# A two-layer hybrid attention kernel on one core: the last pair's reciprocals on another DMA queue, two exponentials always on ACT, three lasting value tiles, one-column Newton steps as tensor_scalar

## The chip, the core and the metric

One Trainium2 chip; the kernel runs on one of its cores. A core has five engines that run side by side and wait for each other through semaphores: PE (TensorE, matmuls), DVE (VectorE, elementwise work), ACT (ScalarE, activations and casts), POOL (GpSimd, elementwise work here) and SP (SyncE, which here only issues DMAs). ACT can issue DMAs too. Each engine takes its instructions strictly in order, and so does each DMA queue's issuer: an instruction that waits holds up all that stand behind it on its engine. The metric is the device time of one execution in microseconds (us), as the median of several runs.

## The reference, cut to what matters

Two transformer layers over 1024 tokens of width 1024, in fp32. Layer 0 mixes with 12 heads of forgetting attention and 4 heads that attend to a memory of 256 rows; layer 1 with 12 latent-attention (MLA) heads and the same 4 memory heads. Each layer ends with an output projection and a convolutional feed-forward network (FFN).

```python
def rmsnorm(x, g):
    xf = x.astype(jnp.float32)
    y = xf * lax.rsqrt(jnp.mean(xf * xf, axis=-1, keepdims=True) + EPS)
    return (y * g.astype(jnp.float32)).astype(x.dtype)
...
    for i in range(DEPTH):
        h = rmsnorm(x, norm_mix[i])
        ...            # p = h @ w_in; o_mix: softmax attention per head, causal
        o_mem = memory_cross(p[..., -MEM_WIDTH:], k_mem, v_mem, mem_q_gain[i], mem_k_gain[i])
        x = x + jnp.concatenate([o_mix, o_mem], axis=-1) @ w_out[i]
        x = x + conv_ffn(rmsnorm(x, norm_ffn[i]), ffn_w_up[i], ffn_conv_w[i], ffn_conv_b[i],
                         ffn_w_down[i])
```

Two pieces matter here. The softmax of a head is exp(score - max) divided by its sum, and the kernel divides after the product with the values. The rmsnorm ahead of each FFN needs one reciprocal square root for every token.

## The kernel before, in words

PE multiplies in a reduced fp32 format (fp32r), so every operand is kept as a high part (the value rounded to fp32r) and a low part (what the rounding lost), and one product is three matmuls. `split` makes the parts: a cast on ACT (L83) and a subtraction on DVE or POOL (L90).

**Attention** (`attention`, 16 heads in 8 pairs per layer). For a group of scores in PSUM (tile `psS`, two buffers), `probs` forms the probabilities: `pf`, the exponential in fp32; `ph`, the same in fp32r; and `plo`, their difference, on POOL. A counter, `pl.turn`, sets who makes `ph`: in four groups of five (layer 0) or five of six (layer 1) ACT computes the exponential twice from PSUM, `ph` first; in the others ACT computes `pf` and DVE casts it. There are 160 groups, 80 in each layer. Each head's values are in `vh` and `vl`; `vh` has a 65th column of ones, which gives the softmax sum as one more output row. In layer 0 `vtile` takes a new pair of tiles for each of the 12 heads from a pool of three and writes the ones anew (L1349).

When both heads of a pair are done, `evacuate` has their outputs in one tile (`oh`) and the sums in `sums`. `norm1` takes the reciprocals (DVE, L387), writes them to DRAM (`rec`, L388) and reads them back as rows spread over 64 partitions each (`rrow`, two DMAs, L391). `norm2` multiplies (L93) and `split_out` makes the high and low parts `oth` and `otl`. All DMAs of `norm1` are issued by SP, behind whatever else stands on its queue.

**Output projection** (`out_proj`). PE multiplies all eight pairs with `wo_w`, the split output weights, which come in as `wo_raw` (two buffers) for one half of the columns and then the other. The first half is arranged so that the last pair comes last. The old x (eight tiles of 512 KB) is loaded at the same time. `add` (L692) adds a result to x, and in the second half calls `ffn.ready`: for each of eight token tiles t, in the order 0, 4, 1, 5, 2, 6, 3, 7, ACT sums the squares, `rsqrt` takes the reciprocal root, and L248 scales.

**rsqrt** works on DVE alone: L216, L217 (a first guess by bit arithmetic), L219, and three Newton steps of two instructions each. With a width of one column, 32 times in the program, they are two `scalar_tensor_tensor`, L222 and L226; each has two tensors in SBUF among its inputs.

**FFN** (`FFN.run`). It transposes the scaled x on PE block by block and splits the blocks (`f_B`, `f_T`), while POOL makes the low parts of weight operands (`f_op`). Then PE is fed steadily.

The order on each engine is made by a scheduler from priorities and its own model of durations. It also hands eight DMA completion counters (lanes, named DMAHW0 to DMAHW7) to the DMAs in turn, over all queues: a DMA waits until the DMA that had its lane before it has landed.

Of the kernel before, what the change touches and what calls it, by code (L numbers as in the profile page):

```python
# [8 lines left out]
F32R = mybir.dt.float32r  # L9
BF16 = mybir.dt.bfloat16  # L10
I32 = mybir.dt.int32
AF = mybir.ActivationFunctionType
OP = mybir.AluOpType
# [4 lines left out]
P = 128  # L18
D = 1024
S = 1024  # L20
NT = S // P
# [53 lines left out]
def hybrid_kernel(ctx: ExitStack, tc: tile.TileContext, A, out):  # L75
    nc = tc.nc
# [4 lines left out]
    def copy(eng, o, i):  # L81
        if eng == "a":
            nc.scalar.copy(o, i)  # L83
        elif eng == "v":
            nc.vector.tensor_copy(o, i)
        else:
            nc.gpsimd.tensor_copy(o, i)

    def sub(eng, o, a, b):
        (nc.vector if eng == "v" else nc.gpsimd).tensor_tensor(o, a, b, op=OP.subtract)  # L90
# [43 lines left out]
    def open_pool(name, bufs, **kw):  # L134
        return tc.alloc_tile_pool(name=name, bufs=bufs, reuse_waits="tile", **kw)
# [7 lines left out]
    rec_d = dram.tile([2, 8, 2, S], F32, name="rec")  # L143
# [62 lines left out]
    def gc(key, n):  # L206
        i = GC[key]
        return g_cols[0:n, i:i + 1]


    def rsqrt(ss, n, width):

        v = small.tile([P, 32], F32, name="rs_v")[:, :width]
        y = small.tile([P, 32], F32, name="rs_y", bufs=6)[:, :width]
        t = small.tile([P, 32], F32, name="rs_t")[:, :width]
        nc.vector.tensor_scalar(v, ss, 1.0 / n, EPS, op0=OP.mult, op1=OP.add)  # L216
        nc.vector.tensor_scalar(y.bitcast(I32), v.bitcast(I32), -0.5, 1597463007.0, op0=OP.mult, op1=OP.add)  # L217
        if width == 1:
            nc.vector.tensor_scalar(v, v, -0.5, None, op0=OP.mult)  # L219
        for i in range(3):  # L220
            if width == 1:
                nc.vector.scalar_tensor_tensor(t, y, y, v, op0=OP.mult, op1=OP.mult)  # L222
            else:
                nc.vector.tensor_tensor(t, y, y, op=OP.mult)
                nc.vector.scalar_tensor_tensor(t, t, -0.5, v, op0=OP.mult, op1=OP.mult)
            nc.vector.scalar_tensor_tensor(y, t, 1.5, y, op0=OP.add, op1=OP.mult)  # L226
        return y

    def sumsq(acc, src, n):
# [3 lines left out]
    class Norm:  # L233
# [5 lines left out]
        def stats(self, *ts):  # L239
            ss = small.tile([P, 4], F32, name="n_ss", bufs=3)  # L240
            for i, t in enumerate(ts):
                sumsq(ss[:, i:i + 1], self.src(t), D)
            y = rsqrt(ss[:, :len(ts)], D, len(ts))
            for i, t in enumerate(ts):
                self.r[t] = y[:, i:i + 1]
# [15 lines left out]

    pl = Pools()
    pl.mem_rows = set()
    pl.turn = 0

    def slot(name="slot", dt=F32):
        return pl.slots.tile([P, 1024], dt, name=name, tag="slot")
# [11 lines left out]
    def attention(L, heads, leads, offset=0, bg=None, fill={}):  # L279
# [30 lines left out]
        def score_units(h, g):  # L310
            half, parts = h.groups[g]
            state = {}

            def part(i):
                if i == 0:
                    state["ps"] = psS()
                ps = state["ps"]
                kt, q0, n, off = parts[i]
                passes = h.passes(kt, q0, n)
                for j, (l, r) in enumerate(passes):  # L320
                    mm(ps[:, off:off + n], l, r, j == 0, j == len(passes) - 1)
                if h.causal and q0 == kt * P:
                    mm(ps[:, off:off + P], idb, mS, False, True)
                if i == len(parts) - 1:
                    pend.append((h, g, *probs(ps, off + n)))

            return [lambda i=i: part(i) for i in range(len(parts))]

        def probs(ps, w):
            pf = pl.pf.tile([P, 1024], F32, name="pf")[:, :w]  # L330
            ph = pl.p.tile([P, 1024], F32R, name="ph")[:, :w]
            plo = pl.p.tile([P, 1024], F32R, name="plo", bufs=pl.nplo)[:, :w]
            pl.turn += 1
            if pl.turn % pl.dve_turn:
                nc.scalar.activation(ph, ps[:, :w], AF.Exp)  # L335
                nc.scalar.activation(pf, ps[:, :w], AF.Exp)  # L336
            else:
                nc.scalar.activation(pf, ps[:, :w], AF.Exp)
                copy("v", ph, pf)
            sub("p", plo, pf, ph.bitcast(F32))  # L340
            return ph, plo

# [42 lines left out]
        def norm1(r):  # L385
            rec = small.tile([16, P], F32, name="rec", bufs=2)
            nc.vector.reciprocal(rec, pl.sum[r])  # L387
            nc.sync.dma_start(rec_d[L, r].rearrange("b (j p) -> (b j) p", p=P), rec)  # L388
            pl.rows[r] = slot("rrow")
            for b in range(2):  # L390
                nc.sync.dma_start(pl.rows[r][64 * b:64 * b + 64, :], rec_d[L, r, b:b + 1, :].to_broadcast([64, S]))  # L391

        def norm2(r, half):
            raw = pl.OT[r]
# [82 lines left out]
    class Head:  # L477
# [6 lines left out]
        def qk_tiles(self):  # L484
            i = pl.nqk % len(pl.qk)
            pl.nqk += 1
            self.QA, self.KA, self.QB, self.KB = T = pl.qk[i]
            if self.causal and i not in pl.rows_set:
                pl.rows_set.add(i)
                for j, a, b in self.const_rows:  # L490
                    copy(self.rows_eng[len(pl.rows_set) > 1], T[j][a:b, :], ones1[a:b, 0:1].to_broadcast([b - a, S]))
# [8 lines left out]
    def load_pair(T, odd, Th, Tl, tl0, tl1, gcol, half):  # L500

        hs = slice(half * 512, half * 512 + 512)
        if odd:
            px = T[0:HD, hs]
        else:
            px = psX()
            for i in range(4):
                t = half * 4 + i
                transpose(px[:, i * P:(i + 1) * P], T[:, t * P:(t + 1) * P], ident)
            copy("v" if pl.layer else "a", T[0:HD, hs], px[HD:P, :])  # L510
            px = px[0:HD, :]
        split_T(px, Th, Tl, tl0, tl1, gcol, HD, half)
# [7 lines left out]
    def dup(dst, src):  # L520
        nc.sync.dma_start(dst.bitcast(F32), src.bitcast(F32))

    class FoxHead(Head):
# [7 lines left out]
        def prep(self):  # L531
            self.qk_tiles()
            o = (self.row % 2) * HD
            q, k = self.p
            QA, KA, QB, KB = self.QA, self.KA, self.QB, self.KB

            def qt(half):
                load_pair(q, self.row % 2, QA, QB, 0, 64, gc("fox_q", HD), half)
                if half:
                    dup(QB[64:128, :], QA[0:64, :])  # L540

            def kt(half):
                if not half:
                    dup(KA[64:66, :], self.cum[self.row:self.row + 1])
                load_pair(k, self.row % 2, KA, KB, 64, 128, gc("fox_k", HD), half)
                if half:
                    dup(KB[0:64, :], KA[0:64, :])

            def vs():
                self.vh, self.vl = pl.vtile()  # L550
                v = self.pv.rearrange("p (t j) -> p t j", t=NT)[:, :, o:o + HD]
                copy("a", self.vh[:, :, 0:64], v)
                sub("p" if self.row < 2 else "v", self.vl, v, self.vh[:, :, 0:64].bitcast(F32))

            return [lambda: kt(0), lambda: qt(0), lambda: kt(1), lambda: qt(1), vs]
# [635 lines left out]
    def pair(c, W, extra=()):  # L1191
# [4 lines left out]
        for t in range(NT):  # L1196
# [17 lines left out]
            for f in extra[:n]:  # L1214
                f()
            del extra[:n]
        r = rsqrt(ss.rearrange("p t i -> p (t i)"), HD, 32).rearrange("p (t i) -> p t i", t=NT)
        for i, T in ((0, q), (2, k)):
            Tv = T.rearrange("p (t h d) -> p t h d", t=NT, h=2)
# [120 lines left out]
    for p in (wp, wr, hp):  # L1340
        p.release()

    qkp, vp = open_pool("qk0", 1), open_pool("v0", 3)
    pl.pf, pl.p, pl.nplo = open_pool("pf0", 2), open_pool("p0", 3), 3

    def vtile():
        vh = vp.tile([P, NT, 65], F32R, name="vh")
        vl = vp.tile([P, NT, 64], F32R, name="vl")
        nc.vector.tensor_copy(vh[:, :, 64], ones1[:, 0:NT])  # L1349
        return vh, vl  # L1350

    pl.vtile = vtile
    pl.OTs = {}

    def split_out(r):
# [3 lines left out]

    pl.split_out = split_out  # L1360
    qk_tiles(qkp, (1, 2, 0), 3)
    pl.ev, pl.dve_turn = "v", 5
    fox = [FoxHead(h, QKV[h // 2][0], QKV[h // 2][1], cum) for h in range(NH)]
    mem = [MemHead(h, 0, mq0) for h in range(NMH)]
    rest = attention(0, fox + mem, [2] * 16, offset=tc.cur_priority - p_last)
# [42 lines left out]
    with early(ffn.p_tail):  # L1408
# [4 lines left out]
        for d in range(ND):  # L1413
            raw = ffn.rp.tile([P, ND, P], F32, name="f_raw").rearrange("p a b -> p (a b)")[:, :N1 + N2]
            nc.sync.dma_start(raw, mwin[d * P:(d + 1) * P, :])
            w = w1.tile([P, 2, N1 + N2], F32R, name="w1_w")
# [221 lines left out]
    def swap():  # L1638
# [3 lines left out]
        for p in (w1, xtp, hp):  # L1642
# [6 lines left out]

    fill = {2: [swap], 5: [lambda: g0.project(2)], 6: [lambda: latents_T(6)],  # L1650
            10: [lambda: g0.project(3), lambda: g0.squares(1), lambda: g0.rotate(1), g0.scale_k, g0.scale_q]}
    pl.ev, pl.dve_turn = "a", 6
    mk = [slot("mK", F32R).rearrange("p (h i) -> p h i", h=NMH) for i in range(2)]

    ORDER = [12, 13, 14, 15, 0, 1, 2, 3, 4, 5, 6, 7, 8, 9, 10, 11]
# [1 line left out]
    heads = [MemHead(r - NH, 1, mq1) if r >= NH else MlaHead(r) for r in ORDER]  # L1657
# [7 lines left out]
    for g in range(1, 6):  # L1665
        p = groups[g].pieces()
# [37 lines left out]
    for j in range(6):  # L1704
        i, x = divmod(t0 + 0.1 + 0.28 * j, 1.0)
# [48 lines left out]
```

## Time and profile before

| | |
|---|---|
| median of 3 runs | 2599.51 us (2595.33 to 2603.27) |
| the profiled execution's own time | 2597.95 us |
| its span, first to last instruction | 2596.2 us |
| PE busy | 2391.8 us, 92% |
| DVE busy | 1819.7 us, 70% |
| POOL busy | 1546.4 us, 60% |
| ACT busy | 1203.2 us, 46% |
| chain that ended last | PE 47%, DVE 34%, ACT 6%, DMA 4% |

PE is busy nearly throughout, so time can be won only where PE stands idle or runs at its lower clock, and there the chain shows who kept it waiting. The idle stretches are few: the start, the two attentions (near 285 to 530 and 1430 to 1800 us), the joints between attention and output projection (near 560 and 1836 us), and the starts of the two FFNs (620 to 680 and 1884 to 1940 us).

### The profile page before, as it was taken

The numbers are of one execution on the slowest core, as the hardware profiler recorded it, in microseconds if no ns is written. First come the engines' busy times: TensorE is split into PE (matmuls) and PEld (weight loads), VectorE is DVE, ScalarE is ACT, GpSimd is POOL, SyncE is SP. The second block draws the span as 40 slices with busy tenths as digits, with TensorE's granted clock in tenths as the row PEclk, the third lists the DMA queues.
The fourth block names the chain that finished last, engine by engine and source line by source line (L and its number), as shares of the span: only waits on it lengthen the run. The fifth ranks groups of instructions, "written<-read, shape, count | busy, mean of one in ns | idle before, by whom it ended". The sixth has DMA issues, their size and how long they took to land.

```text
span 2596.2 us, 32544 instructions
## 1 busy us (share of the span) xinstructions
PE 2391.8 (92%) x11609; PEld 1960.3 (76%) x11609; DVE 1819.7 (70%) x2937; ACT 1203.2 (46%) x2341; POOL 1546.4 (60%) x992
## 2 busy tenths in 40 slices
PE   8999899888999999989998798979989999997999
PEld 7999666667777777767888576757767777776787
DVE  7422788738777677779877868773576776678786
ACT  5544777613444444433454555554254444443343
POOL 1122476723577777678941556665157777776797
PEclk9999899998999999989999899989989999999999
DMA  5210122252222222441330110012312222225221
GB/s 161 59 50 26 34 59 59 61 172 83 66 78 77 90 73 80 180 156 38 106 130 11 34 31 18 19 37 90 132 54 85 73 81 82 82 73 235 81 98 65
DMA packets 163653, 208.91 MB, mean 80 GB/s; under 512 B 11175, under 2 KB 124682, under 8 KB 163490
## 3 DMA queue, kind: packets, MB, share of 16 engines
q1 hardware_dynamic: 162054, 206.63, 25.1%
q8 instruction: 92, 1.51, 0.2%
q14 instruction: 71, 0.58, 0.1%
q10 hardware_dynamic: 1436, 0.18, 0.0%
HBM read 153.34 MB, written 39.98 MB: 74 GB/s over the span
## 4 chain that ended last, share of the span: by engine, by line
PE 47%; DVE 34%; ACT 6%; issue 5%; DMA 4%; POOL 2%; SPq 1%; ACTq 0%; DVEq 0%; POOLq 0%
PE psX L102 19%; PE psS L102 17%; DVE f_v L883 11%; PE psO L102 10%; DVE f_v L93 4%; POOL f_op L90 2%; ACT f_v L881 2%; PE psX L106 2%; ACT f_v L886 2%; DMA rrow<-rec 1%; DVE f_S L781 1%; DVE mA L292 1%; DVE f_S L1071 1%; ACT f_op L83 1%; DVE f_u L849 1%
## 5 line engine op out<-in xcount | busy, mean ns | idle before, releaser
L90 POOL TENSOR_TENSOR f_op<-f_S,f_op 128x512 fp32r<-128x512 f32 x248 | 364.3, 1472 | 287.3 <-ACT f_op L83 287.2
L102 PE MATMUL psS<-f_T,f_op 128*128 128x512 f32 x1584 | 384.6, 394 | 31.1 <-DVE f_u L849 26.1
L90 POOL TENSOR_TENSOR plo<-pf,ph 128x1024 fp32r<-128x1024 f32 (+2 forms) x160 | 313.8, 1972 | 164.6 <-ACT pf L336 99.5
L102 PEld LDWEIGHTS psS<-f_T,f_op 128*128 128x128 f32 x1584 | 293.0, 188 | 106.2 <-issue 38.6
L83 ACT CAST f_op<-f_S 128x512 fp32r<-128x512 f32 x248 | 153.5, 621 | 330.4 <-PE psS L102 143.7
L102 PE MATMUL psX<-f_B,f_op 128*128 128x512 f32 x1260 | 296.0, 389 | 0.0
L102 PEld LDWEIGHTS psX<-f_B,f_op 128*128 128x128 f32 x1260 | 236.5, 188 | 49.2
L90 POOL TENSOR_TENSOR f_op<-f_raw,f_op 128x512 fp32r<-128x512 f32 x146 | 229.1, 1583 | 30.7 <-ACT f_op L83 30.2
L102 PE MATMUL psS<-f_op 128*128 128x512 f32 x960 | 228.1, 396 | 11.2 <-DVE f_x L1128 8.6
L102 PEld LDWEIGHTS psS<-f_op 128*128 128x128 f32 x960 | 182.6, 191 | 53.4 <-DVE f_x L1128 10.3
L883 DVE SCALAR_TENSOR_TENSOR f_v<-f_cg,cw,f_v 128x1023 f32<-128x1023 f32 x88 | 164.0, 1864 | 54.4 <-ACT f_v L881 52.8
L102 PE MATMUL psX<-f_op 128*128 128x512 f32 x666 | 175.7, 406 | 25.9 <-DVE f_op L90 17.8
L90 POOL TENSOR_TENSOR f_op<-f_d,f_op 128x512 fp32r<-128x512 f32 x118 | 175.0, 1502 | 25.4 <-ACT f_op L83 25.1
L102 PEld LDWEIGHTS psX<-f_op 128*128 128x128 f32 x666 | 130.2, 197 | 57.5 <-DVE f_op L90 19.5
L102 PE MATMUL psX<-w_w,hTh 128*128 128x384 f32 (+2 forms) x672 | 167.4, 334 | 2.3 <-ACT hTh L83 2.2
L883 DVE SCALAR_TENSOR_TENSOR f_v<-f_cv,cw,f_v 128x1023 f32<-128x1023 f32 x88 | 151.0, 1716 | 8.7 <-ACT f_v L881 7.3
L335 ACT ACTIVATE ph<-psS 128x1024 fp32r<-128x1024 f32 (+2 forms) x131 | 112.3, 857 | 93.5 <-PE psS L102 84.6
L849 DVE TENSOR_TENSOR f_u<-psS,f_p 128x512 f32<-128x512 f32 x88 | 60.3, 685 | 133.0 <-PE psS L102 133.0
L83 ACT CAST f_op<-f_raw 128x512 fp32r<-128x512 f32 x148 | 90.6, 616 | 116.1 <-issue 42.4
L102 PE MATMUL psX<-KA,QA 66*128 66x128 f32 (+4 forms) x320 | 111.8, 396 | 30.4 <-DVE mA L292 14.1
L90 POOL TENSOR_TENSOR w_w<-w_raw,w_w 128x384 fp32r<-128x384 f32 (+2 forms) x28 | 29.9, 1072 | 176.7 <-ACT w_w L83 176.7
L93 DVE TENSOR_TENSOR f_v<-f_v 128x1024 f32<-128x1024 f32 x44 | 94.8, 2153 | 52.8 <-ACT f_v L886 52.8
(377 smaller groups left out, 5871.1 us busy)
## 6 DMA issues: line engine op xcount, KB each, us to landing
f_raw<-in_ffn_w_up_dram SPq DMA_DIRECT2D x88, 512.0 KB
g<-f_v SPq DMA_DIRECT2D x44, 512.0 KB
f_d<-g SPq DMA_DIRECT2D x36, 512.0 KB
f_d<-in_ffn_w_down_dram SPq DMA_DIRECT2D x36, 512.0 KB
w_raw<-in_fox_w_in_dram SPq DMA_DIRECT2D x48, 192.0 KB
rrow<-rec SPq DMA_DIRECT2D x32, 256.0 KB
wo_raw<-in_w_out_dram SPq DMA_DIRECT2D x32, 256.0 KB
xr<-x SPq DMA_DIRECT2D x16, 512.0 KB
```

The costliest lines, as they stand in the source:

```text
L83: nc.scalar.copy(o, i)
L90: (nc.vector if eng == "v" else nc.gpsimd).tensor_tensor(o, a, b, op=OP.subtract)
L93: (nc.vector if eng == "v" else nc.gpsimd).tensor_tensor(o, a, b, op=OP.mult)
L102: r = nc.tensor.matmul(*a, **k)
L106: r = nc.tensor.transpose(*a, **k)
L292: nc.vector.tensor_reduce(mA[:, q0:q0 + n], px[:, :n * width].rearrange("p (a b) -> p a b", a=n), axis=AX, op=OP.max)
L335: nc.scalar.activation(ph, ps[:, :w], AF.Exp)
L781: nc.vector.tensor_tensor(s[n], b["A21"], b["A22"], op=OP.add)
L849: nc.vector.tensor_tensor(o, x, y, op=OP.add)
L881: nc.scalar.activation(v, src, AF.Identity, bias=cw[:, 3, ch:ch + 1], scale=cw[:, 2, ch:ch + 1])
L883: nc.vector.scalar_tensor_tensor(v[:, k:], src[:, :S - k], cw[:, 2 - k, ch:ch + 1], v[:, k:], op0=OP.mult, op1=OP.add)
L886: nc.scalar.activation(v, v, AF.Silu)
```

## The change

Four edits. In `norm1` the write and the two reads of the pair that ends last (the last head's pair) are issued by ACT instead of SP. `probs` no longer counts turns: ACT always computes `ph` and then `pf`. The value tiles of layer 0 are three lasting pairs, whose ones are written once. With one column, the two instructions of a Newton step are `tensor_scalar`, with the other one-column operands given as per-partition scalars.

```diff
@@ rsqrt
             if width == 1:
-                nc.vector.scalar_tensor_tensor(t, y, y, v, op0=OP.mult, op1=OP.mult)
+
+                nc.vector.tensor_scalar(t, y, y, v, op0=OP.mult, op1=OP.mult)
+                nc.vector.tensor_scalar(y, t, 1.5, y, op0=OP.add, op1=OP.mult)
             else:
                 nc.vector.tensor_tensor(t, y, y, op=OP.mult)
                 nc.vector.scalar_tensor_tensor(t, t, -0.5, v, op0=OP.mult, op1=OP.mult)
-            nc.vector.scalar_tensor_tensor(y, t, 1.5, y, op0=OP.add, op1=OP.mult)
+                nc.vector.scalar_tensor_tensor(y, t, 1.5, y, op0=OP.add, op1=OP.mult)
@@ probs
-            pl.turn += 1
-            if pl.turn % pl.dve_turn:
-                nc.scalar.activation(ph, ps[:, :w], AF.Exp)
-                nc.scalar.activation(pf, ps[:, :w], AF.Exp)
-            else:
-                nc.scalar.activation(pf, ps[:, :w], AF.Exp)
-                copy("v", ph, pf)
+            nc.scalar.activation(ph, ps[:, :w], AF.Exp)
+            nc.scalar.activation(pf, ps[:, :w], AF.Exp)
             sub("p", plo, pf, ph.bitcast(F32))
@@ norm1
-            nc.sync.dma_start(rec_d[L, r].rearrange("b (j p) -> (b j) p", p=P), rec)
+
+            queue = nc.scalar if heads[-1].row // 2 == r else nc.sync
+            queue.dma_start(rec_d[L, r].rearrange("b (j p) -> (b j) p", p=P), rec)
             pl.rows[r] = slot("rrow")
             for b in range(2):
-                nc.sync.dma_start(pl.rows[r][64 * b:64 * b + 64, :], rec_d[L, r, b:b + 1, :].to_broadcast([64, S]))
+                queue.dma_start(pl.rows[r][64 * b:64 * b + 64, :], rec_d[L, r, b:b + 1, :].to_broadcast([64, S]))
@@ FoxHead.prep
-                self.vh, self.vl = pl.vtile()
+                self.vh, self.vl = vtiles[self.row % 3]
@@ layer 0
-    def vtile():
-        vh = vp.tile([P, NT, 65], F32R, name="vh")
-        vl = vp.tile([P, NT, 64], F32R, name="vl")
+    vtiles = [(vp.tile([P, NT, 65], F32R, name=f"vh{i}"), vp.tile([P, NT, 64], F32R, name=f"vl{i}")) for i in range(3)]
+    for vh, vl in vtiles:
         nc.vector.tensor_copy(vh[:, :, 64], ones1[:, 0:NT])
-        return vh, vl
```

The scheduler sets the order anew, and it moves instructions on every engine. Three places are spoken of below. The first is ACT where layer 0's attention passes into the output projection. `oth_5807` is the high part of the last pair but one (pair 6), `oth_5865` that of the last (pair 7); the names in square brackets are the counters that a row waits for. Before:

```order
L83 CAST wo_w_6040<-wo_raw_6038 128x512 [waits DMAHW0_49]
L83 CAST wo_w_6045<-wo_raw_6043 128x512 [waits DMAHW1_49]
L83 CAST wo_w_6050<-wo_raw_6048 128x512 [waits DMAHW2_49]
L83 CAST oth_5807<-oh_5540 128x1024 [waits DVE_49,Activation_49]
L83 CAST wo_w_6055<-wo_raw_6053 128x512 [waits DMAHW2_49]
L83 CAST oth_5865<-oh_5662 128x1024 [waits DMAHW6_49,DMAHW5_49,DVE_49]
```

In the changed kernel the same tiles are named `oth_5780` (pair 6) and `oth_5838` (pair 7) on ACT:

```order
L83 CAST wo_w_6013<-wo_raw_6011 128x512 [waits DMAHW0_49]
L83 CAST wo_w_6018<-wo_raw_6016 128x512 [waits DMAHW1_49]
L386 DMA rec_69<-rec_5688 16x128 [waits DMAHW5_49,DVE_49]
L389 DMA rrow_5691<-rec_69 64x1024 [waits DMAHW5_49,DMAHW3_49]
L389 DMA rrow_5691<-rec_69 64x1024 [waits DMAHW4_49]
L83 CAST oth_5780<-oh_5513 128x1024 [waits Activation_49]
L83 CAST wo_w_6023<-wo_raw_6021 128x512 [waits DMAHW1_49]
L83 CAST wo_w_6028<-wo_raw_6026 128x512 [waits DMAHW2_49]
L83 CAST oth_5838<-oh_5635 128x1024 [waits DVE_49]
```

The cast of pair 6 stood ahead of everything of pair 7's reciprocals; now three DMA issues with their waits stand ahead of it on the same engine. The lanes that the two reads wait for are those of the loads of x on SP at that place in the changed kernel:

```order
L1367 DMA x3_5725<-in_x_dram 128x1024 [waits DMAHW1_49]
L1367 DMA x4_5726<-in_x_dram 128x1024 [waits DMAHW2_49]
L1367 DMA x5_5727<-in_x_dram 128x1024 [waits DMAHW3_49]
L1367 DMA x6_5728<-in_x_dram 128x1024 [waits DMAHW4_49]
L1367 DMA x7_5729<-in_x_dram 128x1024 [waits DMAHW6_49]
```

Each load waits for its own lane's last user, so x5 holds lane 3 and x6 lane 4 when the reads come to them; lane 5 is that of the write of `rec`, which no longer stands on SP.

The second place is PE in the same stretch, where it first asks for pair 6. Before:

```order
L102 MATMUL psO_6012<-wo_w_5793,otl_5670 128x512
L102 MATMUL psS_5811<-wo_w_5798,oth_5807 128x512 x2
L102 MATMUL psS_5812<-wo_w_5798,oth_5807 128x512 x2
L102 MATMUL psX_5934<-wo_w_5798,oth_5807 128x512 x2
L102 MATMUL psX_5960<-wo_w_5798,oth_5807 128x512 x2
```

And on PE in the changed kernel:

```order
L102 MATMUL psO_5985<-wo_w_5766,otl_5643 128x512
L102 MATMUL psS_5784<-wo_w_5771,oth_5780 128x512 x2
L102 MATMUL psS_5785<-wo_w_5771,oth_5780 128x512 x2
L102 MATMUL psX_5907<-wo_w_5771,oth_5780 128x512 x2
L102 MATMUL psX_5933<-wo_w_5771,oth_5780 128x512 x2
```

Nothing moved here: PE asks for pair 6 at the same point of its order, with the same work behind it.

The third place is DVE at the start of layer 0's FFN, around the reciprocal root of the last token tile (t = 7; `f_B11` are low parts that PE's first FFN product needs). Before:

```order
L248 SCALAR_TENSOR_TENSOR x3_5752<-x3_5752,rs_y_6375,f_gain_5759 128x1024
L90 TENSOR_TENSOR f_S2_6475<-f_S1_6474,f_raw_5930 128x512
L216 TENSOR_SCALAR rs_v_6417<-n_ss_6414 128x1
L217 TENSOR_SCALAR rs_y_6418<-rs_v_6417 128x1
L219 TENSOR_SCALAR rs_v_6417<-rs_v_6417 128x1
L90 TENSOR_TENSOR f_B11_6456<-psX_6457,f_B11_6456 128x512
L222 SCALAR_TENSOR_TENSOR rs_t_6419<-rs_y_6418,rs_v_6417 128x1
L226 SCALAR_TENSOR_TENSOR rs_y_6418<-rs_t_6419,rs_y_6418 128x1
...
L90 TENSOR_TENSOR f_B11_6456<-psX_6464,f_B11_6456 128x512
L248 SCALAR_TENSOR_TENSOR x7_5756<-x7_5756,rs_y_6418,f_gain_5759 128x1024
```

And on DVE in the changed kernel, from the scaling of t = 3 on:

```order
L250 SCALAR_TENSOR_TENSOR x3_5725<-x3_5725,rs_y_6348,f_gain_5732 128x1024
L690 TENSOR_TENSOR x7_5729<-x7_5729,psO_6361 128x512
...
L90 TENSOR_TENSOR f_B11_6429<-psX_6430,f_B11_6429 128x512
...
L90 TENSOR_TENSOR f_B11_6429<-psX_6437,f_B11_6429 128x512
L219 TENSOR_SCALAR rs_v_6390<-rs_v_6390 128x1
L90 TENSOR_TENSOR f_B11_6429<-psX_6459,f_B11_6429 128x512
L223 TENSOR_SCALAR rs_t_6392<-rs_y_6391,rs_v_6390 128x1
L224 TENSOR_SCALAR rs_y_6391<-rs_t_6392,rs_y_6391 128x1
...
L90 TENSOR_TENSOR f_B11_6429<-psX_6469,f_B11_6429 128x512
L250 SCALAR_TENSOR_TENSOR x7_5729<-x7_5729,rs_y_6391,f_gain_5732 128x1024
```

The Newton steps have become `tensor_scalar` (L223, L224), the scaling of t = 3 stands right behind its own Newton steps (before, the add of x7 stood between), and two more `f_B11` stand ahead of the Newton steps of t = 7.

## Rows read from the trace of the kernel before

**Rows 1.** Busy time by stage: stretch, length, then PE, PEld, DVE, ACT, POOL, clock, DMA.
```profile
285.00:530.00 245.00, 224.66 (x1205) 162.62 (x1205) 190.64 (x361) 180.15 (x264) 172.51 (x91) 0.95 0.24 57
...
1430.00:1800.00 370.00, 321.39 (x1813) 248.80 (x1812) 273.60 (x612) 202.21 (x308) 228.99 (x146) 0.91 0.12 31
```

**Rows 2.** Timeline of PE at the first joint: start, length, what, idle before and releaser.
```profile
546.51 1.07 PE L102 MATMUL psS<-wo_w,oth 128*128 128x512 f32 x4
...
569.19 2.08 PE L102 MATMUL psS<-wo_w,oth 128*128 128x512 f32 x4 [9.82 <-ACT oth L83]
...
577.20 0.73 PE L102 MATMUL psS<-wo_w,oth 128*128 128x512 f32 x2 [0.28 <-DVE x L692]
```

**Rows 3.** Timeline of PE at the second joint.
```profile
1838.00 3.06 PE L102 MATMUL psX<-wo_w,ot 128*128 128x512 f32 x12 [2.29 <-DVE x L692]
```

**Rows 4.** Waits of PE, 610 to 680 us: total us, times, longest.
```profile
PE psX L106 <- DVE x L248: 4.0, 1, 4.0
PE psO L102 <- DVE f_B L90: 4.0, 1, 4.0
```

**Rows 5.** Waits of PE, 1878 to 1940 us.
```profile
PE psX L106 <- DVE x L248: 2.8, 1, 2.8
```

**Rows 6.** One-column instructions of rsqrt by line: ns minimum, median, maximum.
```profile
L222 DVE SCALAR_TENSOR_TENSOR rs_t<-rs_y,rs_v x96: 201/219/1204, 6.5 to 1894.6; 128x1 f32<-128x1 f32 x96
...
L219 DVE TENSOR_SCALAR rs_v<-rs_v x32: 141/153/155, 6.3 to 1888.8; 128x1 f32<-128x1 f32 x32
```

**Rows 7.** Newton groups of DVE by shape: count, busy us, mean ns, idle before.
```profile
L222 DVE SCALAR_TENSOR_TENSOR rs_t<-rs_y,rs_v 128x1 f32<-128x1 f32 x96 | 29.6, 312 | 2.1
...
L226 DVE SCALAR_TENSOR_TENSOR rs_y<-rs_t,rs_y 128x1 f32<-128x1 f32 x96 | 24.3, 255 | 2.3
```

**Rows 8.** Timeline of DVE at the start of layer 0's FFN, t = 7.
```profile
628.69 1.17 DVE L226 SCALAR_TENSOR_TENSOR rs_y<-rs_t,rs_y 128x1 f32<-128x1 f32 x1
...
633.57 1.19 DVE L226 SCALAR_TENSOR_TENSOR rs_y<-rs_t,rs_y 128x1 f32<-128x1 f32 x1
```

**Rows 9.** Timeline of POOL in the same stretch.
```profile
628.58 2.50 POOL L90 TENSOR_TENSOR f_op<-f_S,f_op 128x512 fp32r<-128x512 f32 x2
```

**Rows 10.** Timeline of DVE: first and last Newton instruction of an earlier tile.
```profile
586.82 0.22 DVE L222 SCALAR_TENSOR_TENSOR rs_t<-rs_y,rs_v 128x1 f32<-128x1 f32 x1
...
587.97 0.16 DVE L226 SCALAR_TENSOR_TENSOR rs_y<-rs_t,rs_y 128x1 f32<-128x1 f32 x1
```

**Rows 11.** DVE groups by shape: count, busy us, mean ns, idle before and releaser.
```profile
L85 DVE CAST ph<-pf 128x384 fp32r<-128x384 f32 x16 | 10.6, 660 | 7.2 <-ACT pf L338 7.2
...
L1349 DVE CAST vh<-ones 128x8 fp32r<-128x8 f32 x12 | 8.9, 752 | 1.8 <-PE psO L102 1.7
...
L85 DVE CAST ph<-pf 128x1024 fp32r<-128x1024 f32 x8 | 6.7, 843 | 0.0
...
L85 DVE CAST ph<-pf 128x896 fp32r<-128x896 f32 x5 | 4.6, 929 | 0.2 <-ACT pf L338 0.2
```

**Rows 12.** Waits of PE in layer 1's attention, 1428 to 1800 us.
```profile
PE psX L102 <- DVE mA L292: 12.3, 7, 5.6
```

**Rows 13.** Second exponential on ACT: ns minimum, median, maximum.
```profile
L336 ACT ACTIVATE pf<-psS x131: 469/917/1047, 287.9 to 1796.8; 128x1024 f32<-128x1024 f32 x56, 128x896 f32<-128x896 f32 x43, 128x384 f32<-128x384 f32 x32
```

**Rows 14.** Timeline of SP's queue at the first joint.
```profile
548.20 0.32 SPq L388 DMA_DIRECT2D rec<-rec  x1
```

**Rows 15.** Chain of waits, 480 to 680 us: start, length, what.
```profile
522.07 4.25 DMA rrow<-rec
...
545.32 8.75 DMA x<-in_x_dram
...
558.25 8.32 DMA rrow<-rec
```

**Rows 16.** Chain of waits at the second joint.
```profile
1809.68 6.58 DMA x<-x
...
1816.27 10.65 DMA rrow<-rec
```

More of the change, by code (lines that the diff above doesn't have):

```diff
@@ L263, in hybrid_kernel @@
     pl.mem_rows = set()
-    pl.turn = 0
     def slot(name="slot", dt=F32):
@@ L1341, in hybrid_kernel @@
         p.release()
-    qkp, vp = open_pool("qk0", 1), open_pool("v0", 3)
+    qkp, vp = open_pool("qk0", 1), open_pool("v0", 1)
     pl.pf, pl.p, pl.nplo = open_pool("pf0", 2), open_pool("p0", 3), 3
-    def vtile():
-        vh = vp.tile([P, NT, 65], F32R, name="vh")
-        vl = vp.tile([P, NT, 64], F32R, name="vl")
+    vtiles = [(vp.tile([P, NT, 65], F32R, name=f"vh{i}"), vp.tile([P, NT, 64], F32R, name=f"vl{i}")) for i in range(3)]
+    for vh, vl in vtiles:
         nc.vector.tensor_copy(vh[:, :, 64], ones1[:, 0:NT])
-        return vh, vl
-    pl.vtile = vtile
     pl.OTs = {}
@@ L1361, in hybrid_kernel @@
     qk_tiles(qkp, (1, 2, 0), 3)
-    pl.ev, pl.dve_turn = "v", 5
+    pl.ev = "v"
     fox = [FoxHead(h, QKV[h // 2][0], QKV[h // 2][1], cum) for h in range(NH)]
@@ L1651, in hybrid_kernel @@
             10: [lambda: g0.project(3), lambda: g0.squares(1), lambda: g0.rotate(1), g0.scale_k, g0.scale_q]}
-    pl.ev, pl.dve_turn = "a", 6
+    pl.ev = "a"
     mk = [slot("mK", F32R).rearrange("p (h i) -> p h i", h=NMH) for i in range(2)]
```

## The prediction

> **What bounds the kernel now.** I read the busy time by stage first, then the waits of PE in the stages where it idles, then the timelines of the engines it waited for. PE is the bound: in layer 0's attention it works 224.66 of 245 us, in layer 1's 321.39 of 370 [rows 1], so 20.3 and 48.6 us of idle time are all that a lighter DVE can win there. At the first joint PE stops for 9.82 us for the high part of pair 7, cast by ACT, and starts again slowly: four matmuls take 2.08 us at 569.19 against 1.07 us at 546.51 [rows 2]. That is half the rate, as at the lower of its two clock levels, after an idle stretch. At the second joint it idles only 2.29 us [rows 3]. At the two FFN starts it stops twice for 4.0 us in layer 0 and first for 2.8 us in layer 1, each time for DVE [rows 4, 5].
>
> The profiled execution took 2597.95 us, 1.56 below the median of 2599.51 and within the three runs. I make the sum on the former and carry it to the latter.
>
> **Newton steps.** What the reader should see in the timeline of DVE is how long the small instructions take. Undisturbed, the six Newton instructions of a tile run from 586.82 to 588.13, 1.31 us, 0.22 and 0.16 us in turn [rows 10]. For t = 7 in layer 0, from the second of the six on, they run from 628.69 to 634.76, with single instructions of 1.17 and 1.19 us [rows 8]: 6.1 us, where the undisturbed five take 1.06. POOL runs two subtractions from 628.58 to 631.08 in the same time [rows 9], and goes on with others. So these instructions, which read two tensors in SBUF, wait for POOL's current instruction. Over the program the 192 took 29.6 + 24.3 = 53.9 us [rows 7], and at 0.22 and 0.16 they would have taken 36.5: 17.4 us are such waits, nearly a third of them in this one tile. L222 goes from a median of 219 to 1204 ns, while L219, a tensor_scalar of the same size in the same sequence, has 155 ns as its maximum over all 32 [rows 6]. The new steps are tensor_scalar, but with per-partition scalars, which L219 has not. Their price is bounded below by L219's 0.153 us and above by L222's undisturbed 0.22, or, if they wait for POOL, by its 1.2. I take 0.22, as nearest in operands, and so about 1.5 us for six: 0.2 more than now where POOL rests, hidden under PE's matmuls for most tiles, and some 4.8 less for t = 7.
>
> By the waits found, layer 0's last two tiles carry about 8 us and layer 1's about 6, which with the rest makes the 17.4. In layer 0 they stand in front of PE's two stops, 8.0 us together [rows 4], and the new order helps: the scaling of t = 3 and two more splits come ahead. Against that, the scaling (two SBUF tensors) moves into POOL's busy stretch and can wait up to 1.25 us, half of the pair at 628.58 [rows 9]. I take 6.5 us. In layer 1 PE's first stop is 2.8 us [rows 5], and I take 4. Bounds: 0, if the new form waits just as long, and 14.
>
> Here a page speaks against the change. By the Trainium skill, VectorE: DVE Perf Modes (Mode 2×_2P), a fp32 tensor_scalar within SBUF uses both of DVE's read ports, and by SBUF — State Buffer (SBUF: two separate sides) such an instruction waits out a GpSimd one that holds the shared pair. By that the gain would be 0 instead of 10.5 us and the sum 2596. The page's condition is an even outermost dimension, and these have one column; by that rule's exception, L219's maximum of 155 ns agrees, but no run here shows the form with per-partition scalars.
>
> **Exponentials and value tiles.** 29 casts leave DVE: 10.6 + 6.7 + 4.6 = 21.9 us, with 7.4 us in which DVE stood waiting for ACT's `pf`, and 9 of 12 writes of ones at 0.752 us, 6.8 [rows 11]. That is 36 us out of 190.64 + 273.60 = 464 of DVE's busy time in the two attentions [rows 1], 7.8%. PE's largest waits there are for DVE (12.3 us for the row maxima in layer 1 alone) [rows 12]. If idle time shrinks in the same share, 7.8% of 68.9 us is 5.4; not all waits are DVE's, so I take 4. Bounds: 0, if other waits end last, and 12, if DVE's 34% of the chain held for these 36 us too. ACT gets 29 more exponentials of 0.92 us at the median [rows 13], 27 us in all. It is busy 180.15 of 245 and 202.21 of 370 us [rows 1], so idle time covers them; without that cover they would cost the 27.
>
> **The first joint.** Here the move costs. ACT takes its instructions in order, and by the changed order the cast of pair 6 stands behind the write of `rec` and both reads. The write waits for the reciprocal and was issued at 548.20 [rows 14]. The reads wait for the write and for lanes 3 and 4, that is for x5 and x6 to land. x3 landed at 545.32 + 8.75 = 554.07, the second read at 558.25 + 8.32 = 566.57 [rows 15]. Between them the queue moved x4 to x7, the FFN gain and one block of FFN weights (512 KB each), two `wo_raw` and two `rrow` (256 KB each): 4 MB in 12.5 us, 1.56 us per 512 KB. So x5 lands near 557.2 and x6 near 558.8, and ACT is held until some 0.5 us later. Queued behind are the casts of pair 6 and the next weights; PE waits for the former. The cast, which before was done when PE came to it at 546.51 [rows 2], would end near 560.3, so PE stops there for almost 14 us. What it did from 546.51 until it ran dry, 569.19 - 9.82 = 559.37, 12.9 us, comes after, then the rest up to 577.20, 8.0 us with its slow start [rows 2]: 581.2, so 4 us later. Pair 7 lands in good time for that: read by 563, multiplied and cast by 567, and PE reaches it near 573. SP's queue loses one weight load ahead of the sums and the write between x5 and x6, about 1 us earlier. I take +3. Bounds: -3, if the lanes were free when the reads come (issued near 552.5, 4.25 us after 548.20, which an undisturbed larger read took [rows 15]; then pair 6 comes near 554.5 and pair 7 before PE needs it), and +6, if x6 lands behind more traffic.
>
> **The second joint.** The reads leave the queue behind the loads of x, where the second took 10.65 us [rows 16]; undisturbed one took 4.25 [rows 15]. By the lanes the second read waits for x3, which follows x2's landing at 1816.26 [rows 16] by 1.56: 1817.8, and lands near 1822.5 rather than 1826.9. But the cast of pair 7 stands behind two weight casts whose loads arrive only near 1826. I take 1.5 of the 2.29 us of idle time [rows 3]; bounds 0 and 2.3. The Trainium skill, DMA: Bandwidth & Descriptors (Issuing engines are not separate DMA queues), says that such transfers interleave on the same engines and only issue time is saved. By that the gain would be 0 and the time 1.5 us longer; the trace before, with everything on one queue, can't show it.
>
> **Sum.** -6.5 - 4 - 4 + 3 - 1.5 = -13: 2597.95 becomes 2585, and the median 2586.5. I forecast 2586. Adding all good ends gives -31, all bad ones +6.
>
> **Rivals.**
> The new steps wait as the old ones did (the page's rule above). For it: no row shows per-partition scalars beside POOL. Against: L219 [rows 6]. The sum is -2.5: 2597. 18 in 100.
>
> The joint costs nothing, because the loads of x land earlier or the lanes are free: -3 instead of +3, with Newton's full 14: 2576. For it: PE is dry there for 9.82 us today [rows 2]. Against: the lanes in the order. 12 in 100.
>
> ACT paces the attention. Each group's PSUM buffer is released by ACT's second pass; in the 29 groups ACT's one pass becomes two, and if PE's next scores wait for that buffer each time, 27 us are added [rows 13] and the 4 are lost: 2586 + 31 = 2617. It decides from some 63% of the 27 on, where the other 9 are eaten and 7.8 more. Against: ACT's idle time [rows 1]. 7 in 100.
>
> The new order of the attention takes back what DVE gives, 0 instead of -4, and the scalings meet POOL, so that Newton brings 5: -3.5, 2595. 10 in 100.
>
> **Numbers.** My forecast has 53 in 100 and its own range 2580 to 2592. What a measurement here can tell from no change is about 0.3%, 7.8 us, so faster means below 2591.7. Faster: 53 + 12 and a part of the edges, 0.67. Same: the first and the last rival, less that part, 0.25. Slower: 0.08. The range of 2573 to 2600 takes in all but the slower case and the far ends of the bounds.
>
> **What would show it.** Right: L223 and L224 never far above 0.22 us with POOL beside them; PE's stops at the FFN starts down to about 1 us each; no DVE cast of `ph`; PE idle from near 546 to 560 for ACT's cast of pair 6, with ACT's queue waiting for x; a read of `rrow` under 5 us at both joints. Wrong: L223 above 1 us beside POOL; PE idle at the first joint below 9 us; more waits of PE for ACT's `pf` in the attention.

## The result, and the profile after

The changed kernel takes **2616.97 us** (median of 4 runs, 2613.6 to 2618.1) against 2599.2 before: a ratio of **1.0065, interval 1.005 to 1.008**. It is slower by 17.8 us, where I forecast 13 less. The profiled execution took 2617.94 us, with a span of 2616.2.

To find the place, I compared the start of each PE matmul with that of the same matmul before (by its tiles and its count). Up to the attention of layer 0 the changed kernel is 1.4 us late; at 545 us it is 8 to 18 us late; in the FFN of layer 0 only 1.5; at the start of layer 1's attention 1.5; at its end 21.8; at the end of the program 20.0. So layer 0's lateness is nearly gone by its FFN (the Newton steps' own gain helps there, see below), and the loss is made within the attention of layer 1. Busy time of the two attentions (columns as in [rows 1]):

```profile
286.90:538.00 251.10, 228.47 (x1203) 167.06 (x1202) 178.47 (x337) 192.90 (x280) 171.03 (x92) 0.93 0.24 57
1431.50:1821.80 390.30, 329.22 (x1815) 256.45 (x1814) 266.96 (x599) 208.46 (x321) 229.88 (x146) 0.89 0.11 29
```

The second row answers to the second of [rows 1]. DVE has 6.6 us less to do (273.60 to 266.96), as planned, and the stage is 20.3 us longer. PE idles 12.5 us more (48.6 to 61.1). It is also busy 7.8 us longer with nearly the same matmuls (1815 against 1813), at a mean granted clock of 0.89 instead of 0.91; no run separates these 7.8 us from the waits. PE does not wait for ACT there: these are its largest waits in that stretch after,

```profile
PE psX L106 <- POOL gk L93: 14.5, 4, 3.8
PE psX L102 <- DVE KB L515: 12.3, 5, 2.8
PE psS L102 <- DMA QA<-mrow: 7.7, 2, 4.4
...
PE psX L102 <- DVE g_vl L90: 4.7, 1, 4.7
```

and the same releasers before:

```profile
PE psX L102 <- DVE KB L517: 8.3, 5, 2.0
PE psX L106 <- POOL gk L93: 6.2, 3, 4.1
PE psS L102 <- DMA QA<-mrow: 5.3, 2, 2.8
...
PE psX L102 <- DVE g_vl L90: 2.9, 1, 2.9
```

The names: per head, `gq` and `gk` are the raw queries and keys, scaled by `rs_y` (16 columns, from the same rsqrt) on DVE, while POOL multiplies the keys' rotary part (`gk<-kr,rs_y`); `KB` is the low part of the keys, `g_vl` that of the values. PE waits 8.3 us more for POOL's part of `gk`, 4.0 more for `KB`, 2.4 more for the row `mrow` that DVE writes and a DMA moves, 1.8 more for `g_vl`: 16.5 us, of which shorter waits, for the row maxima above all, give some back.

**How a removed cast makes the stage longer.** One place, first before. The timelines of POOL and DVE show who runs when (start, length, what, idle before and releaser):

```profile
1543.50 2.10 POOL L90 TENSOR_TENSOR plo<-pf,ph 128x896 fp32r<-128x896 f32 x1 [0.18 <-ACT pf L336]
1548.06 1.00 POOL L90 TENSOR_TENSOR plo<-pf,ph 128x384 fp32r<-128x384 f32 x1 [2.46 <-DVE rs_y L217]
```

```profile
1545.67 0.16 DVE L216 TENSOR_SCALAR rs_v<-g_ss 128x16 f32<-128x16 f32 x1
...
1545.95 0.74 DVE L517 SCALAR_TENSOR_TENSOR KB<-psX,g_cols,KA 96x512 fp32r<-96x512 f32 x1
...
1547.63 0.35 DVE L85 CAST ph<-pf 128x384 fp32r<-128x384 f32 x1
```

The cast of `ph` stands on DVE behind the work that PE waits for, and POOL's subtraction `plo` needs it: POOL is idle for 2.46 us while DVE makes `KB`. (The POOL row names `rs_y`, the next DVE instruction behind the cast.) The same place after:

```profile
1553.15 3.10 POOL L90 TENSOR_TENSOR plo<-pf,ph 128x896 fp32r<-128x896 f32 x2 [0.17 <-ACT pf L335]
```

```profile
1553.80 1.60 DVE L90 TENSOR_TENSOR gq<-rope 128x128 f32<-128x128 f32 x1
1555.32 0.96 DVE L216 TENSOR_SCALAR rs_v<-g_ss 128x16 f32<-128x16 f32 x1
...
1556.40 0.74 DVE L515 SCALAR_TENSOR_TENSOR KB<-psX,g_cols,KA 96x512 fp32r<-96x512 f32 x1
```

ACT has made `ph` and `pf` early, POOL runs both subtractions back to back until 1556.25, and DVE's small instruction takes 0.96 us instead of 0.16, since it waits for the second. It ends 0.03 us behind POOL's, here and in the three steps that follow. `KB` is 0.8 us later, and PE's stop ahead of it is longer, in each of four steps; before, then after:

```profile
1546.75 0.44 PE L102 MATMUL psX<-KA,QA 96*128 96x384 f32 x1 [1.55 <-DVE KB L517]
```

```profile
1557.19 0.69 PE L102 MATMUL psX<-KA,QA 96*128 96x384 f32 x1 [2.35 <-DVE KB L515]
```

The same happens ahead of `g_vl`, near the start of the stage. Before, POOL's `plo` came behind DVE's cast, at 1453.80, and two scalings of `gq` were done by then:

```profile
1449.73 2.23 DVE L93 TENSOR_TENSOR gq<-gq,rs_y 128x768 f32<-128x768 f32 x2
```

After, `plo` runs beside them:

```profile
1451.27 4.39 DVE L93 TENSOR_TENSOR gq<-gq,rs_y 128x768 f32<-128x768 f32 x2
```

```profile
1452.51 2.34 POOL L90 TENSOR_TENSOR plo<-pf,ph 128x1024 fp32r<-128x1024 f32 x1 [0.68 <-ACT pf L335]
```

The second effect is on POOL. It multiplies `gk` twice for each of six pairs of heads; the same pair before and after, each with DVE's timeline beside it:

```profile
1564.20 2.14 POOL L93 TENSOR_TENSOR gk<-kr,rs_y 128x256 f32<-128x256 f32 x2 [1.85 <-DVE rs_y L226]
```

```profile
1563.77 0.27 DVE L305 TENSOR_SCALAR mrow<-psX 8x128 fp32r<-8x128 f32 x1
1563.97 0.24 DVE L226 SCALAR_TENSOR_TENSOR rs_y<-rs_t,rs_y 128x16 f32<-128x16 f32 x2
1564.15 1.72 DVE L93 TENSOR_TENSOR gk<-gk,rs_y 128x512 f32<-128x512 f32 x2
```

```profile
1574.13 4.19 POOL L93 TENSOR_TENSOR gk<-kr,rs_y 128x256 f32<-128x256 f32 x2 [1.57 <-DVE rs_y L228]
```

```profile
1573.97 0.27 DVE L306 TENSOR_SCALAR mrow<-psX 8x128 fp32r<-8x128 f32 x1
1574.17 0.15 DVE L228 SCALAR_TENSOR_TENSOR rs_y<-rs_t,rs_y 128x16 f32<-128x16 f32 x1
1574.25 1.27 DVE L93 TENSOR_TENSOR gk<-gk,rs_y 128x512 f32<-128x512 f32 x2
1575.46 1.81 DVE L93 TENSOR_TENSOR gq<-gq,rs_y 128x768 f32<-128x768 f32 x2
```

The first of the two POOL instructions takes 3.62 us instead of 1.12: it ends 0.5 us after the last of DVE's four scalings. Before, the row `mrow` came ahead of the two last Newton instructions on DVE; now it stands between them, so POOL is released at the first, 0.12 us ahead of the scalings, where before it began 0.05 us behind the first of them (1564.15) and came in between. One of the six pairs was so before, the last, with `mrow` at the same place; four are now, at 2.5 us each. The place of `mrow` is the scheduler's choice, so this second effect comes with the edit through the new order and not from the cast itself.

### The profile page after: what moved, and what is told of

Its sections match the earlier page's. It is cut to its first block, busy times and chain, and to the rows that moved or that the text cites. A ratio compares the mean times of both kernels' runs of the same rounds, so it can differ in the third digit from the quotient of the medians.

```text
span 2616.2 us, 32593 instructions
## 1 busy us (share of the span) xinstructions
PE 2399.9 (92%) x11609; PEld 1968.0 (75%) x11609; DVE 1799.7 (69%) x2899; ACT 1222.4 (47%) x2370; POOL 1552.4 (59%) x992
## 4 chain that ended last, share of the span: by engine, by line
PE 48%; DVE 32%; ACT 6%; issue 4%; DMA 4%; POOL 3%; SPq 0%; ACTq 0%; DVEq 0%; POOLq 0%
PE psX L102 19%; PE psS L102 18%; DVE f_v L881 11%; PE psO L102 9%; DVE f_v L93 4%; POOL f_op L90 2%; ACT f_v L879 2%; PE psX L106 2%; ACT f_v L884 2%; DVE f_S L779 1%; ACT f_op L83 1%; DVE f_u L847 1%; DVE f_S L1069 1%; DMA wo_raw<-in_w_out_dram 1%; DVE f_cg L847 1%
## 5 line engine op out<-in xcount | busy, mean ns | idle before, releaser
L334 ACT ACTIVATE ph<-psS 128x1024 fp32r<-128x1024 f32 (+2 forms) x160 | 133.1, 832 | 96.4 <-PE psS L102 87.3
L335 ACT ACTIVATE pf<-psS 128x1024 f32<-128x1024 f32 (+2 forms) x160 | 132.4, 827 | 1.0 <-POOL plo L90 0.9
```

## The experiments

In the table the last column is the stretch from PE's first product with `g_w` to its first with `wo_w` out of `ot`, us, in the profiled execution (1367.0 to 1775.1 before, 1369.5 to 1796.9 after). The runs of before that were timed beside them have medians of 2599.2 to 2600.7 us.

| run | median us | ratio to before, 95% | layer 1's stretch |
|---|---|---|---|
| before | 2599.2 | 1 | 408.1 |
| changed | 2616.97 | 1.0065 (1.005 to 1.008) | 427.4 |
| e1_exp_act | 2617.89 | 1.0062 (1.0044 to 1.0081) | 426.1 |
| e2_value_tiles | 2600.29 | 1.0001 (0.9986 to 1.0015) | 414.3 |
| e3_newton | 2593.45 | 0.9971 (0.9959 to 0.9982) | 404.6 |
| e4_act_queue | 2605.94 | 1.0023 (1.0008 to 1.0038) | 408.6 |
| e5_exp_l0 | 2602.46 | 1.0007 (0.9991 to 1.0022) | 412.0 |
| e6_after_k_dve | 2609.58 | 1.0029 (1.0015 to 1.0043) | 416.4 |
| e7_before_k_dve | 2602.04 | 1.0013 (0.9996 to 1.0029) | 407.4 |
| e8_queue_l0 | 2602.28 | 1.0004 (0.9989 to 1.0019) | 405.2 |
| e9_after_sub_dve | 2608.40 | 1.0031 (1.0017 to 1.0045) | 413.3 |
| e10_queue_l1 | 2600.81 | 0.9998 (0.9985 to 1.0010) | 408.7 |
| e11_after_both | 2602.17 | 1.0003 (0.9991 to 1.0016) | 408.7 |
| e12_no_queue | 2604.56 | 1.0017 (1.0003 to 1.0030) | 413.5 |

**The four edits, one at a time.**

```diff
-            pl.turn += 1
-            if pl.turn % pl.dve_turn:
-                nc.scalar.activation(ph, ps[:, :w], AF.Exp)
-                nc.scalar.activation(pf, ps[:, :w], AF.Exp)
-            else:
-                nc.scalar.activation(pf, ps[:, :w], AF.Exp)
-                copy("v", ph, pf)
+            nc.scalar.activation(ph, ps[:, :w], AF.Exp)
+            nc.scalar.activation(pf, ps[:, :w], AF.Exp)
```

> The kernel before with one edit, both exponentials on ACT in all 160 groups. In the changed kernel attention of layer 1 lasts 392.5 us against 372.0, with TensorE's matmuls in the same order. Theory: the casts on DVE kept POOL's subtraction behind DVE's two-operand operations; without them the two meet at other places, on the path. Then this run has the whole loss: layer 1's attention 388 to 394 us, the time 2612 to 2622. Rival 1, ACT's in-order DMA queue is the loss: attention of layer 1 stays at 372, the time 2595 to 2601. Rival 2, every edit moves the scheduler's order and the loss is an accident of all four together: attention of layer 1 between 372 and 385 us.

It has the whole loss, in the stretch where the changed kernel has it; both rivals fall. PE's stop at the first joint is 5.7 us, 9.8 before: there the lateness of layer 0 is taken up.

```profile
PE psS L102 <- ACT oth L83: 5.7, 1, 5.7
```

e2, the value tiles (`vtiles[self.row % 3]`, one pool buffer):

> The kernel before with one edit, three persistent pairs of value tiles. Theory (the exponentials carry the loss): within 3 us of 2599, 9 copies of the ones column fewer on DVE. Rival, the persistent tiles tie a head's values to the head three before it and cost the 20 us of layer 1's attention: 2610 or more.

Nothing that can be measured, and 9 copies fewer are worth nothing either. e3, the Newton steps (the two `tensor_scalar` of the diff):

> The kernel before with one edit, the one-column Newton steps as two tensor_scalar. In the changed kernel those 96 steps show no long one, and PE's stops of 4.0 and 4.0 us at the first feed-forward start and 2.8 us at the second are down to 1.0 and 0.8 us. Theory: the gain is this edit's own: 2589 to 2594 (8 us at the two starts). Rival, the gain of the first start in the changed kernel is only the shift of everything ahead of it: 2597 to 2601.

A gain of 0.29%, 7.5 us. The one-column steps never wait for POOL now, in any of the 96 of each line, though 21 and 18 of them run beside a POOL instruction:

```profile
L223 DVE TENSOR_SCALAR rs_t<-rs_y,rs_v x96: 257/272/275, 6.3 to 1912.1; 128x1 f32<-128x1 f32 x96
...
L224 DVE TENSOR_SCALAR rs_y<-rs_t,rs_y x96: 197/214/219, 6.6 to 1912.8; 128x1 f32<-128x1 f32 x96
```

(of the changed kernel; in this run they read 257/273/277 and 197/214/219). PE's waits at the first FFN start, which answer to [rows 4]:

```profile
PE psX L106 <- DVE f_T L90: 3.5, 1, 3.5
...
PE psX L106 <- DVE x L249: 1.2, 1, 1.2
PE psO L102 <- DVE f_B L90: 1.1, 2, 0.8
```

The two stops of 4.0 are 1.2 and 1.1, but a new one of 3.5 us stands behind them. At the second FFN start the first stop is 3.3 us, not shorter than the 2.8 of [rows 5]; a stop of 2.5 us for `f_T` behind it is gone instead. e4, the queue (`queue = nc.scalar if ... else nc.sync`):

> The kernel before with one edit, the last pair's reciprocal row written and read back through ACT's DMA queue. Theory (the exponentials carry the loss): only the joints move: PE's stop at the first joint, 9.8 us before and 8.4 in the changed kernel, is 6 to 10 us, the second joint's 2.3 us goes: 2594 to 2600. What the prediction said, the cast of pair 6 held behind the reads on ACT: 2602. Rival, this edit carries the loss: 2612 or more.

2605.94 is neither the 2594 to 2600 of the theory nor the 2602 of the prediction. ACT's timeline at the first joint shows the mechanism of the prediction: both reads stand on ACT's queue, and the cast of pair 6 behind them.

```profile
548.22 0.36 ACTq L389 DMA_DIRECT2D rec<-rec  x1
555.78 1.15 ACTq L392 DMA_DIRECT2D rrow<-rec  x2
556.97 1.04 ACT L83 CAST oth<-oh 128x1024 fp32r<-128x1024 f32 x1 [13.34 <-issue]
```

What held the reads stands in the chain of waits: the first was released by a load of x (x5), the second followed it without a wait of its own.

```profile
547.17 8.59 DMA x<-in_x_dram
...
555.78 0.50 ACTq L392
...
556.32 0.61 ACTq L392
```

PE stops at 547.1 for 11.0 us, but the second half of the projection starts at 577.53 against 577.20, where I had said 3 later. The four ratios add up to 1.0057, within the interval of the whole change.

**Where the exponentials cost.** Only layer 0's casts moved to ACT (in layer 0 `pl.dve_turn` = 1000):

> The kernel before with both exponentials on ACT in layer 0 alone; layer 1 keeps its casts on DVE. Theory: the loss of the edit (17.7 us with both layers, 2617.9) lies in layer 1, where TensorE has no other work to take over; layer 0's lateness is taken up at the first joint, which waits for transfers: 2597 to 2603. Rival, half of the loss comes from each layer: 2607 to 2611.

No loss that can be measured. By the end of the interval, 0.22%, at most 6 of the 17.7 us are layer 0's; the loss is layer 1's. Next the keys' rotary part, in the changed kernel and, as a control, in the kernel before:

```diff
-                mul("p", self.k[:, ts, :, 64:96], kr[:, ts, None, :].to_broadcast([P, 4, 2, 32]),
+                mul("v", self.k[:, ts, :, 64:96], kr[:, ts, None, :].to_broadcast([P, 4, 2, 32]),
```

> The changed kernel with the 12 multiplications of the keys' rotary part in layer 1 (gk out of kr and rs_y) on DVE instead of POOL. In the changed kernel four of the six POOL pieces that TensorE waits for take 3.62 us, as they begin 0.12 us ahead of DVE's four scalings and get in behind them; in the kernel before it is one of six, the others take 1.12. Theory, this is part of the loss (2.5 us in each of three steps): TensorE's waits for gk fall from 14.5 to 5 us or less and the time is 2607 to 2613. Rival, the waits are not on the path and other DVE work takes their place: 2615 to 2619.

> The control to the run before: the same edit in the kernel before, where five of the six POOL pieces take 1.12 us and TensorE waits 6.2 us for gk. Theory: little to win, 2596 to 2602. Rival, the edit is worth the same in either kernel, whatever the order on DVE: a gain as large as in the changed kernel.

The same edit is worth 7.4 us after (2616.97 to 2609.58; by the ratios 1.0065 to 1.0029, 9.4) and nothing before. PE's waits in layer 1 have, in place of the 14.5 us for POOL's `gk`,

```profile
PE psX L106 <- DVE gk L93: 6.7, 3, 2.3
```

a little above the 5 expected, and 12.3 us for `KB` as in the changed kernel. This takes away the second effect, and of the first the part ahead of `g_vl` with it (2.3 us instead of 4.7). Now the first:

```diff
-            sub("p", plo, pf, ph.bitcast(F32))
+            pl.turn += 1
+            sub("p" if pl.turn % pl.dve_turn else "v", plo, pf, ph.bitcast(F32))
```

with `pl.dve_turn` 6 in layer 1, so that POOL has nothing to do in the 13 groups whose cast stood on DVE.

> The changed kernel with the subtraction of the low part (plo) on DVE instead of POOL in the 13 groups of layer 1 whose cast stood on DVE before; both exponentials stay on ACT in all groups. ACT has the same work as in the changed kernel. Theory: the loss comes from POOL's subtractions that start right behind ACT's second exponential, on top of DVE's chain to KB and to the scalings of gk and gq (PE's stops ahead of KB are 2.35 us in each of four steps, 1.55 before; ahead of the first g_w product 4.75, 2.89 before); without POOL in those groups they are 1.6 and 3 us, layer 1's attention is 8 to 12 us shorter, the time 2604 to 2610. Rival, ACT's added pass in these groups paces the attention: nothing gained, 2615 to 2619.

8.6 us come back (by the ratios 8.8), though ACT has every pass that the changed kernel has: the rival falls. At the place shown above DVE's chain is undisturbed again,

```profile
1548.94 0.16 DVE L216 TENSOR_SCALAR rs_v<-g_ss 128x16 f32<-128x16 f32 x1
...
1549.22 0.73 DVE L517 SCALAR_TENSOR_TENSOR KB<-psX,g_cols,KA 96x512 fp32r<-96x512 f32 x1
...
1550.90 0.55 DVE L90 TENSOR_TENSOR plo<-pf,ph 128x384 fp32r<-128x384 f32 x1
```

and PE's four stops ahead of `KB` are 1.55 to 1.57 us. But the order on DVE turned back with it (`mrow` ahead of both Newton instructions), and POOL's `gk` has its old length:

```profile
1568.65 2.14 POOL L93 TENSOR_TENSOR gk<-kr,rs_y 128x256 f32<-128x256 f32 x2 [0.77 <-DVE rs_y L228]
```

So this run takes away both effects, the second more than the first: PE's waits for `gk` fall from 14.5 to 4.1 us, for `KB` from 12.3 to 9.1, for `g_vl` from 4.7 to 2.6, and those for `mrow`'s DMA grow to 11.8. Its profiled execution (2604.39) lies 4 us under its median, and gets back 14 of the 19 us of the stretch where the medians get back 8.6. The same edit in the kernel before was not run, so how much of this it would win there is open. Both edits together:

> The changed kernel with the 13 subtractions of layer 1 on DVE and the keys' rotary multiplications on DVE. The second alone gave 2609.6. Theory, the two are separate parts of the loss in layer 1: 2598 to 2604, layer 1's attention within 4 us of the kernel before's. Rival, they are the same part: as the better one alone, 2605 to 2610.

The stretch is 408.7, as before the change, and the time is 1.0003, lower than the changed kernel's ratio by as much as the exponentials cost alone (0.0062). But the Newton steps, 0.29% faster alone, are in this kernel too, so some 0.3%, 8 us, is still paid for elsewhere; the queue (0.23% alone) would account for most of that, but its removal below does not bring it. That the parts are separate isn't shown, as the run before mixes them.

**The queue.** Layer 0 alone, layer 1 alone, and the last run with the queue turned back:

> The kernel before with the last pair's reciprocals on ACT's queue in layer 0 alone; both layers cost 5.8 us. What the prediction said: the first joint is 3 us later, 2602. Rival, the first joint moves by 1 us only (11.0 against 9.8 in the run with both layers) and the loss lies in layer 1: 2598 to 2601.

> The kernel before with the last pair's reciprocals on ACT's queue in layer 1 alone. Both layers gave 2605.9 (ratio 1.0023), layer 0 alone a ratio of 1.0004. If the loss lies in layer 1: 2604 to 2608. If the difference of those two runs is scatter: 2599 to 2603.

> The run before, and the last pair's reciprocals back on SyncE's queue. If ACT's queue costs what it cost alone (5.8 us) this is 5 to 6 us under that run, 2592 to 2598 by the theory, which would beat the kernel before and be near the one with the Newton steps alone (2593.5). Rival, the queue costs nothing when the attention ends late: the same time as that run.

Each layer alone costs nothing that can be measured, both cost 0.23%, and taking the queue's edit out of e11 moved it from 1.0003 to 1.0017, no gain, where I had expected 5 to 6 us. These can't all be the price of the queue. In the profiled execution of e4 (2602.27, 3.7 us under its median) PE's matmuls are 4.3 us late at the end; 0.5 of these stand behind the first joint, 0.4 more come at the second, and 2.4 come near 1340 us, between the two attentions, where nothing of the queue stands. Each edit also moves the scheduler's order elsewhere: the stretch of layer 1 lies between 404.6 and 414.3 us in seven kernels whose edits leave its casts alone. That is one execution of each, so what of it is order and what is the difference between executions isn't shown. The queue's 5.8 us stay unexplained. Of all kernels the one with the Newton steps alone is the fastest, below both (0.9971).

## Why the prediction was wrong, point by point

- **Exponentials, the step that failed.** "If idle time shrinks in the same share ... I take 4. Bounds: 0 ... and 12"; measured alone +17.7 us. I costed the DVE time that the casts free and the ACT time that they need, and let PE's idle time follow DVE's load. DVE's load did fall, by 12.2 us in layer 0 and 6.6 in layer 1. What I left out is the third engine: the casts also decided when POOL's subtraction could start. Removing them freed POOL to run on top of the DVE work on PE's path, and the only loss that I had priced was ACT's 27 us, set aside by its idle time. In place of the 4 us of gain the runs show longer stops of PE in layer 1: in the changed kernel 5.8 us more ahead of `KB` and `g_vl` (POOL beside DVE's work), 8.3 ahead of `gk` (the new order) and 2.4 ahead of `mrow`, whose cause I did not follow. That DVE and POOL hold each other up was in my own rows, priced for the Newton steps alone [rows 8, 9].
- **The slow rival had the time and not the reason.** "ACT paces the attention" gave 2617, the measured time, by luck: PE waits for ACT nowhere in layer 1's attention after, and e9 wins 8.6 us with ACT's work unchanged. The fourth rival (a new order takes back what DVE gives) is nearer: the order on DVE is the second effect, at 2.5 us a step, where I had the order at 4 us altogether.
- **Layer 0** lost nothing that can be measured (e5). In the changed kernel its attention ends late, but at the first joint PE stops anyway until transfers land, for 8.39 us where it was 9.82 [rows 2], and the second half of the projection starts 5.2 us late. 3.7 of these go at the FFN start, where the Newton steps alone bring 4.4: their gain covers what the joint leaves. In e5, without the new steps, 4 us are left behind the joint in the profiled execution (3.2 us above its median).
- **Newton steps**: right in mechanism, 3 us too large in size. The sum had 10.5 us; alone they bring 7.5 (6.7 between medians). In the profile of e3 the first FFN start gives 4.4 us, where I took 6.5, and the second 2.9, where I took 4, because waits for the next DVE results (`f_T`, 3.5 us) come behind. My sign, stops of about 1 us, came at the first start and not at the second (3.3 us). The steps take 272 and 214 ns, 486 for the two where I had 440, and far from POOL's 1.2 us. The rival that they wait like the old ones falls with a longest of 275 ns (277 in e3). The page cited against it, the Trainium skill, VectorE: DVE Perf Modes (Mode 2×_2P), asks for an outermost dimension above one that is even, or odd and equal on both sides; I gave only the first half. The runs agree with it: a `tensor_scalar` of 16 columns on DVE did wait (0.96 us above), of one column none did, with per-partition scalars or with constants (L219, 156 ns at most after).
- **First joint**: the cast is held behind the reads as foretold, the size was off: +0.3 instead of +3. In e4 x5 had landed by 555.76, 1.4 us before my 557.2, and the second read did not wait for x6 as it does in the changed kernel's order, so the cast began at 556.97 and not near 559.3, and PE's stop was 11.0 us, not almost 14. In the changed kernel the second read does wait for x6 (561.27), but PE comes there 8 us late and stops for 8.39, under the 9 us that I had named as a sign of being wrong.
- **Second joint**: -1.5 did not come; layer 1's queue alone has a ratio of 0.9998, and the changed kernel stops there for 1.37 and 0.95 us, together as long as the 2.29 of [rows 3].
- **Value tiles**: part of the 4 us; alone nothing (1.0001).

## What to carry to other kernels

Ask of each instruction you take away not only what it costs, but whom it holds back: a cast at the end of one engine's queue can keep a third engine off a shared resource while the work that counts runs. Where two engines delay each other, look at which of their instructions meet, not at their sums of busy time; less work on one can mean more waiting on the path. A bound of "no loss" on an edit needs a look at every engine that the edit releases earlier. And lateness ahead of a stop that ends with a transfer can in part be taken up there (here 8 us before the first joint, 5.2 behind it), so price the same edit separately in each stage.

## What the runs showed of the hardware that I had not expected

Between DVE and POOL the one that loses can wait for more than one instruction. POOL's `gk`, recorded as starting 0.12 us ahead of DVE's four scalings, took 3.62 us and ended 0.5 us after the last of them, while the four ran in 3.0 us. Recorded 0.05 us behind the first it took 1.12, and DVE's second scaling waited (1.10 us instead of 0.67). The fastest of the 12 POOL instructions on `gk` takes 0.61 us, so by these records POOL waited in both orders. The Trainium skill, SBUF — State Buffer (SBUF: two separate sides), says that the instruction that starts first holds the shared ports for its whole length; the recorded starts here don't agree with that, and a lead of a tenth of a microsecond went with 2.5 us more at each meeting. Nor does the wait need two tensors: a `tensor_scalar` of 16 columns took 0.96 us where 0.16 is usual, and up to 1.5 in other places of the same line, before and after.
